# Hybrid decoder trunk on one core: a triangular solve's stores on ScalarE's queue, the bias table's columns from one wider load, x first in the first half

## The chip, the cores and the metric

The kernel runs on one core of a Trainium2 chip. The metric is the device time of one launch in microseconds (us), the median of several runs. A core has five engines that work side by side, each through its own list of instructions in order: TensorE (PE in the profile), VectorE (DVE), ScalarE (ACT), GpSimd (POOL) and SyncE (SP), which here does nothing but issue DMAs. An instruction whose input is not there holds up everything behind it on its engine, and that goes for a DMA issue too.

## The reference, cut to what matters

Two layers over 1024 tokens of width 1024. Each layer normalises x, projects it once, and splits the columns among four mixers; their outputs are gated, joined, projected, normalised and added to x.

```python
for i in range(DEPTH):
    h = rms_norm(x, g_pre[i])
    proj = h @ w_in[i]
    ...
    kc = nsa_compress(k_cmp, ...); vc = nsa_compress(v_cmp, ...)   # silu(flat @ w1) @ w2
    y_a = nsa_attention(q, kc, vc, ..., rel_bias)
    y_b = spatial_gating(u, v, ...)
    y_c = conv_module(glu_a, glu_b, ...)
    y_d = rwkv7_time_mix(token_shift(rw, mu), ...)      # a scan over tokens
    mix = concat([y_a * silu(z_a), y_b * silu(z_b), y_c * silu(z_c), y_d * silu(z_d)])
    x = x + rms_norm(mix @ w_out[i], g_post[i])
    x = x + sigmoid(x @ ple_gate[i]) * (p[i] @ ple_proj[i])
```

The recurrence of `rwkv7_time_mix` is computed here in chunks of 64 tokens. Each chunk needs the inverse of a 64 by 64 triangular matrix per head; that inverse is the "solve" of this document.

## The kernel before

**Halves and steps.** Each layer is done in two halves of 512 tokens, so there are four passes, called A, B, C and D here (layer 0 first and second half, layer 1 first and second half). `run` walks through a string of letters for each pass (`ORDER`, L32): X loads x, i and e do the embedding (`embed_in`, `embed_out`), H the norm, B `setup_late`, F and R the recurrence's front and its solve, N the front of the attention with the compression (`nsa_front`), r the recurrent steps, G, T and C the convolution, a, b, c, d the gates, s the spatial gating, A a tile of attention. The letters give the order in which the code is written; a tile scheduler then fixes the order of every engine's list, by priority and by its own idea of times.

**Weights.** Nearly all of TensorE's work is `mm3` (L169): three products of 128x512 for every 128x128 block of weights, with the high and low parts of both factors. Four blocks make a granule (12 products). `split_w` (L150) brings a granule: SP loads it to `ws` (L155), ScalarE rounds it to `wh` (L161), GpSimd subtracts for `wl` (L163), and where `keep` is set SP stores `wl` to memory (L166), so that the second half of the same layer loads it (L160) rather than have GpSimd do it again. All of this has three buffers, so SP can be about three granules ahead of TensorE.

**The solve** (`rwkv_solve`, L453). The triangular blocks go to a scratch tensor `Nd` and come back in another layout (L474, L479). VectorE then inverts 16x16 blocks by 15 pairs of small instructions (L487, L489), and the blocks below them by 16 more pairs (L509, L511). After the first group ScalarE copies a transposed `XT` (L495), and `put` (L497) stores 8 pieces in `Xd`; after the second it copies `WT` (L513), and `put` stores 8 more. All 16 stores are issued by SP (L499). `rwkv_tri` (L533) loads the finished chunks back (L539, SP) and begins with the products of L543.

**The compression** (`compress_out`, L866) is run beside the solve. Its products (L874) read eight tiles of `nsa_w1`, which SP loads to `ld` tiles (L834). There are five `ld` buffers, so five tiles come early and the last three can be loaded only when products have freed a buffer; the loads stand where the scheduler put them in SP's list.

**The bias table.** `setup_late` (L106) builds a table of biases by distance. It writes a scratch row, reads it back once as 128 overlapping rows of 256 (`hk`, L131), and reads every 16th element of it by four more DMAs (`hc`, L135), 128x17 single elements of 4 bytes each.

Of the kernel before, what the change touches and what calls it, by code (L numbers as in the profile page):

```python
# [16 lines left out]
TH = 512  # L17
NT = 4
KT = 8
# [9 lines left out]
C_ID, C_MA, C_ML, C_SUM, C_FAR, C_HB, C_FLAG, C_HS, C_N = 0, 128, 320, 384, 416, 544, 672, 673, 675  # L29
S_ANTI, S_OH, S_N = 0, 128, 256  # L30
RROW = 2128
ORDER = ("iXeHFBRNrGabscdnAAATCy",  # L32
         "HAFRNGrbsaAAAAdcniOexTgCy",
         "HFRNrGabscdniOxeAAgAATyC",
         "HFRNGraAbsAAnAcdOTxgCy")
# [6 lines left out]
class Trunk:  # L42
# [63 lines left out]
    def setup_late(self):  # L106
        nc, a = self.nc, self.a
        zz = self.t([128, 1024], "r4")
        nc.vector.memset(zz, 0.0)
        for i in range(2):  # L110
            for q in range(2):
                nc.sync.dma_start(self.Xd[i][:, q * 1024:q * 1024 + 1024], zz)

        rs = self.dram.tile([4, RROW], F32, name="rscratch")
        st = self.t([128, S_N], "r4")
        nc.sync.dma_start(st[:, :S_N], a["cst"][:, C_N:C_N + S_N])
        rb = self.const([32, 4], "rb")
        nc.sync.dma_start(rb, a["rel_bias"])
        row = self.t([128, 1024], "r4")
        row2 = self.t([128, 1024], "r4")  # L120
        nc.vector.memset(row[:4, :977], 0.0)
        nc.vector.memset(row2[:4, :1023], NEG)
        pr = self.ps("pt")
        nc.tensor.matmul(pr[:4, :128], rb, st[:32, S_OH:S_OH + 128], start=True, stop=True)
        mid = self.t([128, TH], "ld")[:4, :128]
        nc.vector.tensor_copy(mid, pr[:4, :128])
        nc.sync.dma_start(rs[:, :977], row[:4, :977])
        nc.sync.dma_start(rs[:, 977:1105], mid)
        nc.sync.dma_start(rs[:, 1105:2128], row2[:4, :1023])
        hk = self.t([128, 4, 256], "r4")  # L130
        nc.sync.dma_start(hk, bass.AP(tensor=rs.tensor, offset=rs.offset + 849,  # L131
                                      ap=[[1, 128], [RROW, 4], [1, 256]]))
        hc = self.t([128, TH], "ld")[:, :68].rearrange("p (a b) -> p a b", a=4)
        for h in range(4):
            nc.sync.dma_start(hc[:, h], bass.AP(tensor=rs.tensor, offset=rs.offset + 848 + h * RROW,  # L135
                                                ap=[[1, 128], [16, 17]]))
        for p in range(2):
            pj = self.ps("pt")
            nc.tensor.matmul(pj, st[:, S_ANTI:S_ANTI + 128],
                             hk[:, 2 * p:2 * p + 2, :].rearrange("p a b -> p (a b)"), start=True, stop=True)  # L140
            nc.scalar.copy(self.T[:, 2 * p:2 * p + 2, :].rearrange("p a b -> p (a b)"), pj)
        nc.vector.memset(self.TC[:, :, :53], 0.0)
        nc.vector.memset(self.TC[:, :, 70:], NEG)
        pj = self.ps("pt")
        nc.tensor.matmul(pj[:, :68], st[:, S_ANTI:S_ANTI + 128], hc.rearrange("p a b -> p (a b)"),
                         start=True, stop=True)
        nc.vector.tensor_copy(self.TC[:, :, 53:70], pj[:, :68].rearrange("p (a b) -> p a b", a=4))


# [303 lines left out]
    def rwkv_solve(self):  # L453
        nc = self.nc
        Nd, Xd = self.Nd[self.nq % 2], self.Xd[self.nq % 2]
        self.Xcur = Xd
        self.nq += 1
        self.AT, self.BKt, self.XF = {}, {}, {}
        for c in range(4):
            self.rwkv_ab(c)  # L460
            for j in range(2):
                nc.sync.dma_start(Nd[:, c * 256 + j * 128:c * 256 + j * 128 + 128].rearrange("p (h t) -> p h t", h=2),
                                  self.AT[c][0:64, j, :, 64 * j:64 * j + 64])
        ma = self.c[0:64, C_MA:C_MA + 64].unsqueeze(1).to_broadcast([64, 2, 64])
        for c in range(4, 8):
            Nc = self.t([128, 256], "q3", bufs=1)[:64].rearrange("p (a b c) -> p a b c", a=2, b=2)
            for e, pA in enumerate(self.a_blocks(1, c - 4, False)):
                nc.vector.tensor_mul(Nc[:, :, e], pA[0:64, :128].rearrange("p (h c) -> p h c", h=2), ma)
            nc.sync.dma_start(Nd[:, c * 256:c * 256 + 256].rearrange("p (h t) -> p h t", h=4),
                              Nc.rearrange("p a b c -> p (a b) c"))  # L470
        LB = self.t([128, 256], "q1", bufs=1).rearrange("p (a b) -> p a b", a=16)
        XB = self.t([128, 256], "q2", bufs=1).rearrange("p (a b) -> p a b", a=16)
        for b in range(4):
            nc.sync.dma_start(LB[b * 32:b * 32 + 32], bass.AP(tensor=Nd.tensor, offset=Nd.offset + b * 16 * 2048 + b * 16,  # L474
                                                              ap=[[64, 32], [2048, 16], [1, 16]]))
        L2 = self.t([128, 512], "l2", bufs=1).rearrange("p (a b) -> p a b", a=32)
        for b in range(4):
            p = b // 2
            nc.sync.dma_start(L2[b * 32:b * 32 + 32], bass.AP(  # L479
                tensor=Nd.tensor, offset=Nd.offset + p * 32 * 2048 + p * 32 + 16, ap=[[64, 32], [2048, 32], [1, 16]]))  # L480
        nc.gpsimd.memset(XB, 0.0)
        nc.gpsimd.affine_select(out=XB, in_=XB, compare_op=OP.not_equal, fill=1.0, base=0,
                                pattern=[[1, 16], [-1, 16]], channel_multiplier=0)
        tmp = self.t([128, 256], "q3", bufs=1)
        for t in range(1, 16):
            tv = tmp[:, :t * t].rearrange("p (a b) -> p a b", a=t)
            nc.vector.tensor_mul(tv, LB[:, 0:t, t].unsqueeze(1).to_broadcast([128, t, t]),  # L487
                                 XB[:, 0:t, 0:t].rearrange("p j a -> p a j"))
            nc.vector.tensor_reduce(XB[:, t, 0:t], tv, axis=AX.X, op=OP.add)  # L489
        XW = self.t([128, 32, 8], "q4", bufs=1)  # L490
        for b in range(4):
            p, g = divmod(b, 2)
            nc.vector.tensor_copy(XW[b * 32:b * 32 + 32, 0:16], XB[p * 64:p * 64 + 32, :, g * 8:g * 8 + 8])
        XT = self.t([128, 256], "q1", bufs=1).rearrange("p (a b) -> p a b", a=16)
        nc.scalar.copy(XT, XB.rearrange("p t j -> p j t"))  # L495

        def put(b, q, r0, c0, src, rows, cols):  # L497
            o = Xd.offset + (q * 64 + b // 2 * 32 + r0) * 2048 + b // 2 * 32 + c0
            nc.sync.dma_start(bass.AP(tensor=Xd.tensor, offset=o, ap=[[64, 32], [2048, rows], [1, cols]]),  # L499
                              src[b * 32:b * 32 + 32])  # L500

        for b in range(4):
            d = b % 2 * 16
            put(b, 0, d, d, XB, 16, 16)
            put(b, 1, d, d, XT, 16, 16)
        for t in range(16):
            n = 16 + t
            tv = tmp[:, :8 * n].rearrange("p (j a) -> p j a", j=8)
            nc.vector.tensor_mul(tv, L2[:, 0:n, t].unsqueeze(1).to_broadcast([128, 8, n]),  # L509
                                 XW[:, 0:n].rearrange("p a j -> p j a"))  # L510
            nc.vector.tensor_reduce(XW[:, n], tv, axis=AX.X, op=OP.add)  # L511
        WT = self.t([128, 128], "q5", bufs=1).rearrange("p (a b) -> p a b", a=8)
        nc.scalar.copy(WT, XW[:, 16:32].rearrange("p t j -> p j t"))  # L513
        for b in range(4):
            put(b, 0, 16, b % 2 * 8, XW[:, 16:32], 16, 8)
            put(b, 1, b % 2 * 8, 16, WT, 8, 16)
# [671 lines left out]
    def run(self):  # L1188
        prev = conv = att = None
        for l in range(2):  # L1190
            self.layer_setup(l)
            for h in range(2):
                self.h = h
                self.keep = h == 0
                mixd = self.mixd = self.mix_dram[h]
                for step in ORDER[2 * l + h]:
                    if step == "A":
# [13 lines left out]
                    elif step == "i":  # L1211
                        pT = self.embed_in()
                    elif step == "e":
                        self.embed_out(pT)
                    elif step == "X":
                        self.xs = [self.load_x(k) for k in range(KT)]
                    elif step == "n":
                        self.rwkv_norm()
                    elif step == "N":
# [106 lines left out]
```

## Time and profile before

| | |
|---|---|
| three runs | 1885.58, 1890.34, 1898.15 us; median 1890.34 |
| profiled execution, its own time | 1888.04 us |
| its span, first to last instruction | 1886.3 us |
| TensorE busy | 1700.9 us, 90% |
| VectorE, ScalarE, GpSimd busy | 1204.5, 798.0, 383.6 us |
| TensorE's mean granted clock | 0.934 of full speed |

The profile is one execution. In a timeline each row has its start, its duration, the engine, the line of the kernel, the operation, what it writes and reads, how many were merged, and in brackets how long the engine stood idle before it and what it waited for. PE is TensorE; SPq and ACTq are DMA issues of SyncE and ScalarE. The granted clock has two levels, 1.2 GHz (0.5 in the rows) and 2.4 GHz (1.00); a mean in between is a stretch with both.

### The profile page before, as it was taken

The page shows a single profiled execution, that of the slowest core. Times are in us where ns is not written, and L with a number is a line of the kernel's source. Part 1 is how long each engine was busy: PE and PEld are TensorE (multiplying, and loading weights), DVE is VectorE, ACT ScalarE, POOL GpSimd, SP SyncE. Part 2 cuts the span into 40 slices and gives each one's busy share as a digit, 9 for nine tenths or more (in the row PEclk, how much of TensorE's full clock was granted, in tenths as well). Part 3 has the DMA queues.
Part 4 walks back from the last instruction along what each step waited for, and adds up shares of the span by engine and source line. Part 5 has one row for each costly group of instructions (what it writes and reads, how often), then busy time and mean ns, then how long its engine had stood idle before and what let it go on. Part 6 is the DMA issues. An engine that isn't in the chain of part 4 may idle for free. (4 is left out here: it accounts for less than half of the span.)

```text
span 1886.3 us, 29258 instructions
## 1 busy us (share of the span) xinstructions
PE 1700.9 (90%) x10068; PEld 1252.8 (66%) x10068; DVE 1204.5 (64%) x3217; ACT 798.0 (42%) x1801; POOL 383.6 (20%) x319
## 2 busy tenths in 40 slices
PE   5795998999699999998877989999988999998998
PEld 4563676677576777775654768776766767675777
DVE  3456788765688764656566982557558877546353
ACT  4331233554223466544321334556432446554453
POOL 2222234000001023132331341200000011232333
PEclk8897798899899999998997989999998999989999
DMA  7645354324753443574464448672475424114554
GB/s 246 144 132 138 109 178 128 104 78 112 175 150 110 123 146 101 162 217 127 124 158 111 137 133 256 227 222 82 115 169 152 140 74 130 50 40 129 179 181 137
DMA packets 372492, 265.42 MB, mean 141 GB/s; under 512 B 93676, under 2 KB 305648, under 8 KB 372344
## 3 DMA queue, kind: packets, MB, share of 16 engines
q1 hardware_dynamic: 359288, 250.98, 46.7%
q10 hardware_dynamic: 13056, 12.59, 2.0%
q8 instruction: 79, 1.29, 0.3%
q14 instruction: 69, 0.57, 0.1%
HBM read 193.63 MB, written 69.86 MB: 140 GB/s over the span
## 5 line engine op out<-in xcount | busy, mean ns | idle before, releaser
L171 PE MATMUL mm<-aT,wh 128*128 128x512 f32 (+1 forms) x1304 | 540.2, 416 | 9.6 <-ACT aT L260 5.3
L172 PE MATMUL mm<-aT,wh 128*128 128x512 f32 (+1 forms) x1304 | 537.0, 412 | 3.8 <-DVE aT L261 3.2
L173 PE MATMUL mm<-aT,wl 128*128 128x512 f32 (+1 forms) x1304 | 535.4, 411 | 0.0
L161 ACT CAST wh<-ws 128x512 fp32r<-128x512 f32 (+2 forms) x388 | 236.7, 611 | 494.1 <-PE mm L172 313.3
L163 POOL TENSOR_TENSOR wl<-ws,wh 128x512 fp32r<-128x512 f32 (+1 forms) x220 | 292.0, 1329 | 702.1 <-ACT wh L161 647.1
L171 PEld LDWEIGHTS mm<-aT,wh 128*128 128x128 f32 (+1 forms) x1304 | 251.5, 193 | 70.8 <-ACT aT L260 7.8
L172 PEld LDWEIGHTS mm<-aT,wh 128*128 128x128 f32 (+1 forms) x1304 | 251.8, 193 | 62.7 <-DVE aT L261 11.0
L173 PEld LDWEIGHTS mm<-aT,wl 128*128 128x128 f32 (+1 forms) x1304 | 251.6, 193 | 51.1 <-issue 1.7
L697 DVE SCALAR_TENSOR_TENSOR cv<-cv,cw,cv 128x512 f32<-128x512 f32 x240 | 191.8, 808 | 4.0
L1035 ACT ACTIVATE r<-s,sma 128x512 f32<-128x512 f32 (+3 forms) x192 | 105.7, 554 | 52.7 <-DVE sma L1033 51.8
L976 ACT COPY pt<-pt 128x512 f32<-128x512 f32 (+1 forms) x152 | 80.4, 529 | 106.6 <-PE pt L973 106.2
L611 POOL TENSOR_TENSOR q<-SB,gc 128x256 f32<-128x256 f32 x28 | 22.9, 816 | 475.1 <-DVE SB L624 174.1
L973 PE MATMUL pt<-cst,r 128*128 128x128 f32 x528 | 102.9, 293 | 3.2 <-DVE r L1040 2.8
L981 PE MATMUL pv<-pt,vs 128*64 128x128 f32 x1056 | 93.4, 291 | 3.7 <-ACT pt L976 3.5
L981 PEld LDWEIGHTS pv<-pt,vs 128*64 128x64 f32 x1056 | 55.8, 138 | 57.3 <-ACT pt L976 47.5
L973 PEld LDWEIGHTS pt<-cst,r 128*128 128x128 f32 x528 | 61.2, 143 | 38.4 <-issue 23.9
L1025 DVE CUSTOM_DVE_ANT_0 s<-s,T 128x256 f32<-128x256 f32 (+1 forms) x144 | 54.2, 377 | 46.4 <-PE s L1006 45.8
L1005 PE MATMUL s<-kv,qs 128*128 128x512 f32 (+2 forms) x192 | 74.6, 390 | 3.0 <-ACT r L1035 2.9
L874 PE MATMUL pt<-ld,t 128*32 128x128 f32 x256 | 13.0, 330 | 67.0 <-DMA ld<-in_nsa_w_dram 67.0
L1040 DVE TENSOR_SCALAR r<-r,sma 128x640 f32<-128x640 f32 (+7 forms) x128 | 68.3, 533 | 0.7
L1006 PE MATMUL s<-kv,qs 128*128 128x512 f32 (+2 forms) x192 | 65.7, 347 | 0.0
L1037 DVE TENSOR_TENSOR sma<-sma 128x1 f32<-128x1 f32 x64 | 13.7, 214 | 70.1 <-ACT r L1035 69.9
(328 smaller groups left out, 2687.2 us busy)
## 6 DMA issues: line engine op xcount, KB each, us to landing
ws<-in_w_in_dram SPq DMA_DIRECT2D x232, 256.0 KB, 3.2
wl<-low SPq DMA_DIRECT2D x164, 256.0 KB, 2.7
low<-wl SPq DMA_DIRECT2D x148, 256.0 KB, 2.1
ws<-in_ple_gate_dram SPq DMA_DIRECT2D x64, 256.0 KB, 3.0
ws<-in_w_out_dram SPq DMA_DIRECT2D x60, 256.0 KB, 2.9
ped<-ot ACTq DMA_DIRECT2D x32, 256.0 KB, 4.2
ld<-in_nsa_w_dram SPq DMA_DIRECT2D x32, 256.0 KB, 3.1
ld<-ped SPq DMA_DIRECT2D x32, 256.0 KB, 3.8
```

Source lines behind the costliest of these rows:

```text
L161: nc.scalar.copy(hi[:, :cols], st[:, :cols])
L163: nc.gpsimd.tensor_sub(lo[:, :cols], st[:, :cols], hi[:, :cols].bitcast(F32))
L171: nc.tensor.matmul(out, lh, rh, start=first, stop=False, skip_group_check=shared)
L172: nc.tensor.matmul(out, lh, rl, start=False, stop=False, skip_group_check=shared)
L173: nc.tensor.matmul(out, ll, rh, start=False, stop=last, skip_group_check=shared)
L697: nc.vector.scalar_tensor_tensor(ac, xg[j][:, k:k + TH], cw[:, j * 31 + k:j * 31 + k + 1], ac, op0=OP.mult, op1=OP.add)
L973: nc.tensor.transpose(pt[:, o:o + 128], P[e][:, (b + x - b0) * 128:(b + x - b0) * 128 + 128], self.ident)
L976: nc.scalar.copy(PT[:, :n], pt[:, :n])
L981: nc.tensor.matmul(acc[e], w.VS[hh][:, tt, br], PT[:, o:o + 128], start=False, stop=br == 1 and b + x == i, skip_group_check=True)
L1005: nc.tensor.matmul(p[:, :n], w.QS[hd][:, qs], w.KH[br, hh][:, c0 * 128:c1 * 128], start=True, stop=False)
L1035: nc.scalar.activation(P[:, o:o + wd], p[:, c:c + wd], AF.Exp, bias=ng[:, 0:1], accum_out=den[:, x:x + 1])
L1040: nc.vector.tensor_scalar(P[:, :n], P[:, :n], r, None, op0=OP.mult)
```

## The change

The 64 stores of the four solves are issued by ScalarE. `hk` is loaded one element wider, both tables are read from it, and the four loads of single elements are gone. In pass A the step X stands before i, its loads are given high priority, and `embed_out` runs with `keep` off, so that the low parts of `ple_proj` are not stored, and are computed by GpSimd each time.

```diff
-ORDER = ("iXeHFBRNrGabscdnAAATCy",
+ORDER = ("XieHFBRNrGabscdnAAATCy",
...
-        hk = self.t([128, 4, 256], "r4")
-        nc.sync.dma_start(hk, bass.AP(tensor=rs.tensor, offset=rs.offset + 849,
-                                      ap=[[1, 128], [RROW, 4], [1, 256]]))
-        hc = self.t([128, TH], "ld")[:, :68].rearrange("p (a b) -> p a b", a=4)
-        for h in range(4):
-            nc.sync.dma_start(hc[:, h], bass.AP(tensor=rs.tensor, offset=rs.offset + 848 + h * RROW,
-                                                ap=[[1, 128], [16, 17]]))
+        hk = self.t([128, 4, 257], "r4")
+        nc.sync.dma_start(hk, bass.AP(tensor=rs.tensor, offset=rs.offset + 848,
+                                      ap=[[1, 128], [RROW, 4], [1, 257]]))
...
-                             hk[:, 2 * p:2 * p + 2, :].rearrange("p a b -> p (a b)"), start=True, stop=True)
+                             hk[:, 2 * p:2 * p + 2, 1:257], start=True, stop=True)
...
-        nc.tensor.matmul(pj[:, :68], st[:, S_ANTI:S_ANTI + 128], hc.rearrange("p a b -> p (a b)"),
-                         start=True, stop=True)
+        nc.tensor.matmul(pj[:, :68], st[:, S_ANTI:S_ANTI + 128], hk[:, :, 0:257:16], start=True, stop=True)
...
-            nc.sync.dma_start(bass.AP(tensor=Xd.tensor, offset=o, ap=[[64, 32], [2048, rows], [1, cols]]),
-                              src[b * 32:b * 32 + 32])
+            nc.scalar.dma_start(bass.AP(tensor=Xd.tensor, offset=o, ap=[[64, 32], [2048, rows], [1, cols]]),
+                                src[b * 32:b * 32 + 32])
...
                     elif step == "e":
+                        self.keep = False
                         self.embed_out(pT)
+                        self.keep = h == 0
                     elif step == "X":
-                        self.xs = [self.load_x(k) for k in range(KT)]
+                        with self.tc.high_priority():
+                            self.xs = [self.load_x(k) for k in range(KT)]
```

The scheduler orders the whole program anew, so the lists differ in many places. Three of them follow, all in pass A's solve; passes B, C and D look alike. In the changed kernel's rows the line numbers are 5 lower.

SP's list in the kernel before: the second eight of the solve's stores (`Xd<-q`, L499; the first eight stand just above) and the last three loads of the compression's weights (`ld<-in_nsa_w_dram`, L834):

```order
L834 DMA ld_1309<-in_nsa_w_dram 128x4x128
L499 DMA Xd_85<-q_217_966 32x16x8
L499 DMA Xd_85<-q_219_1013 32x8x16
L499 DMA Xd_85<-q_217_966 32x16x8
L499 DMA Xd_85<-q_219_1013 32x8x16
L499 DMA Xd_85<-q_217_966 32x16x8
L499 DMA Xd_85<-q_219_1013 32x8x16
L499 DMA Xd_85<-q_217_966 32x16x8
L499 DMA Xd_85<-q_219_1013 32x8x16
L834 DMA ld_1315<-in_nsa_w_dram 128x4x128
L834 DMA ld_1321<-in_nsa_w_dram 128x4x128
```

SP's list in the changed kernel, from the last loads of the solve's input (`l<-Nd`, now L474) on:

```order
L474 DMA l_214_913<-Nd_83 32x32x16 x2
L829 DMA ld_1296<-in_nsa_w_dram 128x4x128
L161 DMA low_1894<-wl_1891 128x512
L150 DMA ws_1954<-in_w_in_dram 128x4x128
L829 DMA ld_1302<-in_nsa_w_dram 128x4x128
L161 DMA low_1918<-wl_1915 128x512
L150 DMA ws_1974<-in_w_in_dram 128x4x128
L829 DMA ld_1308<-in_nsa_w_dram 128x4x128
L747 DMA ld_2174<-in_sgu_wT_dram 128x4x128
```

The three loads have moved ahead of everything that waits for the solve; nine granules' loads (`ws`), two of them in these rows, stand between the solve's input and the first `x<-Xd` (L534).

ScalarE's list before, from `XT`'s copy to `WT`'s:

```order
L495 COPY q_218_971<-q_214_921 128x256
L161 CAST wh_1927<-ws_1925 128x512
L161 CAST wh_1947<-ws_1945 128x512
L161 CAST wh_1969<-ws_1967 128x512
L513 COPY q_219_1013<-q_217_966 128x128
```

ScalarE's list in the changed kernel around `WT`'s copy (L508) and the second group of stores (L494); the first group stands further up between three casts of granules:

```order
L156 CAST wh_2021<-ws_2019 128x512
L508 COPY q_218_1000<-q_216_953 128x128
L494 DMA Xd_85<-q_216_953 32x16x8
L494 DMA Xd_85<-q_218_1000 32x8x16
L494 DMA Xd_85<-q_216_953 32x16x8
L494 DMA Xd_85<-q_218_1000 32x8x16
L156 CAST wh_2045<-ws_2043 128x512
L494 DMA Xd_85<-q_216_953 32x16x8
L494 DMA Xd_85<-q_218_1000 32x8x16
L494 DMA Xd_85<-q_216_953 32x16x8
L494 DMA Xd_85<-q_218_1000 32x8x16
L156 CAST wh_2065<-ws_2063 128x512
```

The copy now stands three casts of granules later in the list than before, and the casts of the next two granules stand behind it and the stores.

VectorE's list before, at the end of the solve:

```order
L509 TENSOR_TENSOR q_216_935<-l_215_926,q_217_966 128x240
L511 TENSOR_REDUCE q_217_966<-q_216_935 128x8
L509 TENSOR_TENSOR q_216_935<-l_215_926,q_217_966 128x248
L511 TENSOR_REDUCE q_217_966<-q_216_935 128x8
L682 SCALAR_TENSOR_TENSOR cv_1834<-t_382_1837,mm_1880 128x512
```

VectorE's list in the changed kernel at the same place (L692 is a tap of the convolution, L697 before; L504 and L506 are L509 and L511):

```order
L692 SCALAR_TENSOR_TENSOR cv_3357<-cv_1821,cw_99,cv_3357 128x512
L504 TENSOR_TENSOR q_215_922<-l_214_913,q_216_953 128x240
L692 SCALAR_TENSOR_TENSOR cv_3357<-cv_1821,cw_99,cv_3357 128x512
L506 TENSOR_REDUCE q_216_953<-q_215_922 128x8
L692 SCALAR_TENSOR_TENSOR cv_3357<-cv_1821,cw_99,cv_3357 128x512
L504 TENSOR_TENSOR q_215_922<-l_214_913,q_216_953 128x248
L692 SCALAR_TENSOR_TENSOR cv_3357<-cv_1821,cw_99,cv_3357 128x512
L506 TENSOR_REDUCE q_216_953<-q_215_922 128x8
```

Taps and other work of the convolution and the compression have come between the last pairs of the solve.

On TensorE the number of weight products (L171 to L173) between the place at which pass A's compression waits and the first product on the solve's result (L543) is 0 before and 82 now; in B it is 0 and 78, in C 0 and 82, in D 48 and 90. In B only the first two of L543's products stand at that place.

## Rows read from the trace of the kernel before

**Rows 1.** The page: busy us, share, instructions; GB/s in 40 slices.

```profile
PE 1700.9 (90%) x10068; PEld 1252.8 (66%) x10068; DVE 1204.5 (64%) x3217; ACT 798.0 (42%) x1801; POOL 383.6 (20%) x319
...
GB/s 246 144 132 138 109 178 128 104 78 112 175 150 110 123 146 101 162 217 127 124 158 111 137 133 256 227 222 82 115 169 152 140 74 130 50 40 129 179 181 137
```

**Rows 2.** Who waited for whom: us in total, times, longest.

```profile
ACT q L513 <- DVE q L511: 45.1, 4, 12.8
...
PE pt L874 <- DMA ld<-in_nsa_w_dram: 67.0, 12, 12.2
```

**Rows 3.** Timeline of TensorE in pass A: start us, us, what.

```profile
161.25 0.39 PE L173 MATMUL mm<-aT,wl 128*128 128x512 f32 x1
...
163.97 0.39 PE L173 MATMUL mm<-aT,wl 128*128 128x512 f32 x1
174.85 0.66 PE L874 MATMUL pt<-ld,t 128*32 128x128 f32 x8 [10.49 <-DMA ld<-in_nsa_w_dram]
187.69 0.66 PE L874 MATMUL pt<-ld,t 128*32 128x128 f32 x8 [12.19 <-DMA ld<-in_nsa_w_dram]
...
190.69 0.69 PE L543 MATMUL rp<-x,at 64*64 64x64 f32 x8
```

**Rows 4.** Timeline of SP's DMA issues over the same stretch.

```profile
153.58 1.16 SPq L479 DMA_DIRECT2D l<-Nd  x2
...
171.97 0.43 SPq L834 DMA_DIRECT2D ld<-in_nsa_w_dram  x1
180.61 3.92 SPq L499 DMA_DIRECT2D Xd<-q  x8
184.63 0.95 SPq L834 DMA_DIRECT2D ld<-in_nsa_w_dram  x2
...
186.30 0.84 SPq L539 DMA_DIRECT2D x<-Xd  x2
```

**Rows 5.** Timeline of VectorE: the solve's last instruction in passes A to D.

```profile
180.17 0.41 DVE L511 TENSOR_REDUCE q<-q 128x8 f32<-128x248 f32 x1
...
505.38 0.41 DVE L511 TENSOR_REDUCE q<-q 128x8 f32<-128x248 f32 x1
...
994.10 0.41 DVE L511 TENSOR_REDUCE q<-q 128x8 f32<-128x248 f32 x1
...
1421.59 0.41 DVE L511 TENSOR_REDUCE q<-q 128x8 f32<-128x248 f32 x1
```

**Rows 6.** Windows: length, each engine's busy us (instructions), clock, DMA share, GB/s.

```profile
164.40:209.80 45.40, 22.07 (x111) 13.72 (x111) 25.93 (x55) 4.64 (x12) 7.01 (x6) 0.55 0.48 120
498.30:523.90 25.60, 10.94 (x51) 6.91 (x51) 12.89 (x27) 2.91 (x9) 1.54 (x2) 0.53 0.48 120
978.80:1015.40 36.60, 13.99 (x80) 8.39 (x81) 21.01 (x47) 3.52 (x10) 5.38 (x5) 0.53 0.53 128
1410.40:1428.40 18.00, 7.46 (x42) 4.73 (x42) 14.18 (x32) 2.09 (x7) 0.61 (x1) 0.62 0.57 118
83.00:100.60 17.60, 7.78 (x31) 5.11 (x31) 4.77 (x12) 5.37 (x9) 4.16 (x3) 0.61 0.80 238
```

**Rows 7.** Timeline of SP, then of TensorE, at the bias table.

```profile
65.10 12.47 SPq L135 DMA_DIRECT2D ld<-rscratch  x4
...
92.86 1.86 PE L386 MATMUL rp<-cst,t 128*128 128x2 f32 x8 [9.82 <-ACT t L383]
```

**Rows 8.** Timeline of TensorE at the start: the first norm.

```profile
31.92 1.86 PE L268 MATMUL mm<-onec,qa 128*128 128x1 f32 x8 [8.28 <-DVE qa L301]
```

**Rows 9.** Groups on the page: line, engine, operation, count, busy us, mean ns, idle before.

```profile
L161 ACT CAST wh<-ws 128x512 fp32r<-128x512 f32 (+2 forms) x388 | 236.7, 611 | 494.1 <-PE mm L172 313.3
L163 POOL TENSOR_TENSOR wl<-ws,wh 128x512 fp32r<-128x512 f32 (+1 forms) x220 | 292.0, 1329 | 702.1 <-ACT wh L161 647.1
...
L697 DVE SCALAR_TENSOR_TENSOR cv<-cv,cw,cv 128x512 f32<-128x512 f32 x240 | 191.8, 808 | 4.0
```

**Rows 10.** Timeline of TensorE: a link of the recurrent steps.

```profile
281.19 0.46 PE L602 MATMUL c<-q,xf 64*64 64x64 f32 x8 [2.01 <-DVE q L599]
```

## The prediction

> **What bounds the kernel now.** I read the page first, then the list of waits, then timelines of single stretches. TensorE is busy 90% of the span [rows 1], so what can be won is its idle time, some 185 us, and the time it works at the lower clock. The list of waits names one cause that stands out: TensorE waited 67.0 us, 12 times, for tiles of `nsa_w1` [rows 2].
>
> The timelines of pass A tell why. TensorE works without a break to 164.4, then waits 10.49 and 12.19 us for two tiles that L874 multiplies [rows 3]. SP had issued the solve's input at 153.6 and the first of the three late tiles only at 172.0, the other two at 184.6 [rows 4]. What stands between in its list are the stores of the solve. The second eight are issued at 180.61, right behind VectorE's last instruction of the solve (180.17 + 0.41) [rows 4, 5]. So the loads waited for VectorE, with which they have nothing to do, because SP issues in order. TensorE waits in its turn and drops to the lower clock.
>
> Windows from the stall's start to the clock's return, for A to D, give the size [rows 6]. Length less PE busy is 45.4 - 22.1 = 23.3, 25.6 - 10.9 = 14.7, 36.6 - 14.0 = 22.6 and 18.0 - 7.5 = 10.5 us, 71.1 us idle in all. The busy parts, 22.1, 10.9, 14.0 and 7.5 us, lie nearly all behind the stall, where the granted clock was 0.50; at full clock half of that time would do, so the clock costs up to 27.2 us more.
>
> A smaller place lies in the front. The four loads of single elements hold SP for 12.47 us from 65.1; the weights behind them come late and TensorE waits 9.82 us at 83 [rows 7]. That window has 9.8 us idle and 7.8 us busy, mostly at 0.50: 9.8 + 3.9 = 13.7 us [rows 6].
>
> **The stores on ScalarE: what goes.** SP's list in the changed kernel has the three tiles behind the solve's input and ahead of what waits for the solve, so they need only a free buffer, which TensorE's first products on the tiles give. I count the waits for `nsa_w1` as gone.
>
> What is late next is the solve itself. In pass A the first product on its result (L543) starts at 190.69 [rows 3], 10.1 us behind VectorE's end at 180.58: copy, eight stores (3.92 us of issue), their landing, and the load of `x` [rows 4, 5]. On ScalarE the same eight stores stand behind `WT`'s copy with one cast of weights among them (0.61 us [rows 9]). ScalarE's price of issuing such a store isn't in the trace. The nearest row is SP's, 3.92 / 8 = 0.49 us; from nothing to double that is 0 to 8 us per solve, and I take 0.49. So 10.7 us from VectorE's end to L543.
>
> VectorE's end moves too. In its new list the last pairs of A are mixed with six taps of the convolution and six smaller instructions: 6 x 0.81 [rows 9] = 4.9, and some 2 us for the others (an estimate from L511's 0.41 us [rows 5], since they are as small), 6.8 us; in B and D seven taps, 7.6 us. If all of it fell into gaps of the pairs it would be 0, if each waited for its input more; I take the full sum. L543 can then start at 180.6 + 6.8 + 10.7 = 198.1 in A; with the ends of the other passes [rows 5], 505.8 + 7.6 + 10.7 = 524.1 in B, 994.5 + 6.8 + 10.7 = 1012.0 in C, and 1422.0 + 7.6 + 10.7 = 1440.3 in D.
>
> Against this stands the work that TensorE now has before L543. From the old stall on these are 82, 78, 82 and 90 weight products. Twelve of them take 163.97 - 161.25 = 2.72 us [rows 3], 0.227 each, so 18.6, 17.7, 18.6 and 20.4 us. The compression's own small products add an estimated 3.8 us (three groups of 0.66 [rows 3], and as much again), and 1.2 us in B for a group of the solve's. TensorE is ready at 164.4 + 18.6 + 3.8 = 186.8 in A, 498.3 + 17.7 + 5.0 = 521.0 in B, 978.8 + 18.6 + 3.8 = 1001.2 in C and 1410.4 + 20.4 + 3.8 = 1434.6 in D. It waits 11.3, 3.1, 10.8 and 5.7 us, 30.9 us in all. In A and C part of that comes a little sooner, because the casts of the last granule before L543 stand behind `WT`'s copy; that splits the wait and does not add to it.
>
> Idle time saved: 71.1 - 30.9 = 40.2 us. The work pulled forward is paid for by leaving less work for later; nothing is done twice.
>
> Clock: three waits over 5 us stay. The one wait of this size in the front cost 3.9 us of clock, so I leave 3 x 3.9 = 11.7 of the 27.2 us and save 15.5. The bounds are 0, if the clock falls for as long as now, and 27.2, if it doesn't fall.
>
> What is queued behind the new waits: on ScalarE the casts of the following granules. ScalarE already waits 45.1 us in its four copies L513 [rows 2]; that copy now stands three granules later, about when VectorE ends. The stores themselves add no wait, as each stands behind a copy that waited for the same tile.
>
> A rule of the Trainium skill speaks against this part: "DMA: Bandwidth & Descriptors", section "Issuing engines are not separate DMA queues", says that DMAs from any engine end on the same 16 DMA engines, and that spreading them saves only the issuing sequencer's time. By it alone 64 x 0.49 = 31 us of SP's time is saved, none of it on TensorE's path, and the stores are worth nothing. The trace agrees that issue time is small but shows that here SP's list is held by waits, which the rule leaves out [rows 4].
>
> **The bias table.** The four loads go, and with them the 12.47 us of SP. The wide load is one element wider per row; I cost it at nothing. The new slice of `hk` feeds one product of 68 columns. Saved 13.7 us; at least 9.8 if the clock falls for another reason. What comes next there is TensorE's own chain through ScalarE and VectorE.
>
> **x first.** The eight loads of x (2 MB) now stand ahead of those of p, which feed TensorE's first products. At the 246 GB/s of the first slice [rows 1] that is 8 us of later start. The cover is the 8.28 us for which TensorE waits in front of the first norm, because x is late [rows 8]: the norm's products stand behind the embedding in TensorE's list, so they start as early as before, at about 32 us, and the wait moves to the front. I take 0, with bounds of 8 us lost and 8 us gained. With `keep` off GpSimd subtracts for 8 more granules, 8 x 1.33 = 10.6 us [rows 9], and 16 DMAs of 256 KB go. GpSimd is busy 20% of the span [rows 1], one subtraction takes half of a granule's 2.72 us of products, and the loads run three granules ahead: 0, at worst 10.6.
>
> **Sum.** 40.2 + 15.5 + 13.7 = 69.4 us. The profiled execution took 1888.0 us, 2.3 under the median of 1890.3, so 1888.0 - 69.4 = 1818.6, and I say 1819.
>
> **Rivals.**
> 1. The waits move to ScalarE. If VectorE ends its mixed chain later than I think, ScalarE stands in L513 as it does now, 11.3 us on average, the casts behind it starve TensorE, and each pass wins nothing. For it: TensorE has only three granules of weights ahead. Against it: 82 products take twice that wait. Only the front's gain is left: 1888.0 - 13.7 = 1874. 0.05. The same 1874 follows if the loads were late for another reason than SP's list, full DMA engines for one, so that the stores save issue time alone; the engines' share of busy time is about half in these windows [rows 6], so 0.02. This second case is the one that the rule of the Trainium skill quoted above would lead to.
> 2. Slower: the recurrent steps run dry. The 82 products and more that now come before the steps no longer fill them. Each step has three links from TensorE over a copy and back; where few products stand between, the link costs 2.01 us [rows 10]. With 32 steps there are 96 links. It decides against the change from 70 / 96 = 0.73 us more per link; at 2 us in half of them it is 96 us, 1819 + 96 = 1915. For it: a scheduler's times were wrong about the solve. Against it: the new list pulls other work (spatial gating, the first attention tile) between the links. 0.04.
> 3. No wait is left at the solves and the clock holds: 71.1 + 27.2 + 13.7 = 112, 1776. For it: B is nearly there. Against it: VectorE's end is fixed by 31 pairs that nothing shortens. 0.12.
>
> **How the numbers follow.** My forecast has 0.77. Its range follows from its unknowns: the clock 15 down and 12 up, ScalarE's issue 8 in three passes, x first and the subtractions some 8 each, hardly all one way: 1786 to 1852. It leaves out most of rivals 1 to 3. About 1%, 19 us, is what a measurement of this kernel can tell from no change. Rival 1 with its 0.07 is 0.7% under before, so it counts as no change; rival 2 is slower; the rest is faster: 0.89, 0.07, 0.04.
>
> **What would show it.** Right: no wait of L874 for `nsa_w1`; a wait of 3 to 11 us at the first product on the solve's result in each pass; taps of the convolution inside the solve on VectorE; the 9.82 us at 83 gone; the first norm near 32 us. Wrong: ScalarE waiting over 10 us in L513's copy with TensorE idle behind its casts; idle time spread over the links of the steps; the first norm at 40 us.

## The result and the profile after

The changed kernel takes 1814.57 us (median of 4 runs, 1811.26 to 1819.83) against 1888.39 us (4 runs). The ratio is 0.9603, 95% interval 0.956 to 0.9645: 75 us faster. 1819 was predicted, with 1786 to 1852 as the range. The profiled execution is the slowest of the four: 1819.83 us, span 1818.1 us, 68.2 us shorter than before.

The head of the page of the changed kernel answers to [rows 1]:

```profile
span 1818.1 us, 29200 instructions
PE 1687.8 (93%) x10068; PEld 1242.4 (68%) x10068; DVE 1208.3 (66%) x3217; ACT 797.0 (44%) x1801; POOL 402.8 (22%) x327
```

TensorE's work is the same 10068 instructions. Span less busy was 1886.3 - 1700.9 = 185.4 us and is 130.3 now: 55.1 us less idle. Its busy time fell by 13.1 us with the same work: that is the clock, whose mean rose from 0.934 to 0.961.

The list of waits of the changed kernel (who waited for what: us in all, times, longest), against [rows 2]:

```profile
PE mm L166 <- ACT t L1060: 18.9, 1, 18.9
...
PE pt L869 <- DMA ld<-in_nsa_w_dram: 15.9, 9, 4.3
ACT wh L156 <- DMA Xd<-q: 15.6, 8, 3.0
...
PE rp L538 <- DMA x<-Xd: 9.6, 4, 4.7
...
ACT q L508 <- DVE q L506: 7.2, 3, 3.3
...
PE pt L135 <- DMA r<-rscratch: 6.2, 1, 6.2
```

Four readings (the first row, 18.9 us, is the start, which stands later because x is loaded first; it was 9.5 before). TensorE's waits for `nsa_w1` (L874, now L869) fell from 67.0 to 15.9 us. Its wait for the solve's result (L538) has appeared, 9.6 us. ScalarE's wait in `WT`'s copy (45.1 us before) has not grown but shrunk to 7.2, as the copy stands later in its list. Its casts wait 15.6 us behind the stores that it issues now.

Windows over the four solves, from the first wait to the clock's return, as [rows 6] has them of before, and under them the stretches at the lower clock that lie in them (length, PE busy, PEld, DVE, ACT, POOL, granted clock, DMA share, GB/s):

```profile
150.40:192.00 41.60, 30.80 (x142) 22.89 (x142) 40.46 (x71) 10.04 (x21) 16.05 (x11) 0.84 0.67 171
466.90:496.00 29.10, 26.63 (x140) 20.30 (x140) 27.81 (x57) 8.27 (x18) 1.26 (x2) 1.00 0.89 239
924.50:973.70 49.20, 39.75 (x179) 28.36 (x178) 44.10 (x79) 11.25 (x23) 16.95 (x12) 0.79 0.62 162
1348.90:1362.70 13.80, 10.50 (x53) 6.72 (x53) 11.62 (x29) 2.49 (x8) 1.49 (x2) 0.63 0.83 233
157.90:164.70 6.80, 5.10 (x23) 3.35 (x23) 6.46 (x15) 1.10 (x3) 2.16 (x2) 0.50 0.83 237
185.20:192.00 6.80, 4.55 (x23) 3.28 (x24) 6.68 (x12) 0.62 (x1) 1.27 (x1) 0.50 0.53 147
929.30:932.70 3.40, 2.81 (x7) 1.65 (x5) 3.19 (x7) 0.50 (x1) 1.37 (x1) 0.50 0.97 235
936.10:939.50 3.40, 3.40 (x12) 2.25 (x11) 3.33 (x10) 0.38 (x2) 1.58 (x1) 0.50 0.49 133
960.00:973.70 13.70, 12.71 (x60) 8.44 (x60) 9.61 (x19) 1.83 (x3) 3.24 (x2) 0.50 0.35 108
1352.50:1362.70 10.20, 9.30 (x43) 6.14 (x43) 8.30 (x21) 1.87 (x7) 1.49 (x2) 0.50 0.71 210
```

Length less PE busy is 10.8, 2.5, 9.5 and 3.3 us in A to D, 26.0 in all, where it was 71.1. At the lower clock TensorE worked 37.9 us (the six lower rows), which costs half of it, 19 us, where it was 27.2. So the solves give 45.1 us of idle time and 8.2 of clock. Up to the solve of pass A, `XT`'s copy there stands at 150.7 instead of 162.6, which is 11.9 us for the front. 45.1 + 8.2 + 11.9 = 65.2 of the 68.2 us; the last 3 are scattered.

### The profile page after: what moved, and what is told of

Its sections match the earlier page's. It is cut to its first block, busy times and chain, and to the rows that moved or that the text cites. A ratio compares the mean times of both kernels' runs of the same rounds, so it can differ in the third digit from the quotient of the medians.

```text
span 1818.1 us, 29200 instructions
## 1 busy us (share of the span) xinstructions
PE 1687.8 (93%) x10068; PEld 1242.4 (68%) x10068; DVE 1208.3 (66%) x3217; ACT 797.0 (44%) x1801; POOL 402.8 (22%) x327
## 5 line engine op out<-in xcount | busy, mean ns | idle before, releaser
L158 POOL TENSOR_TENSOR wl<-ws,wh 128x512 fp32r<-128x512 f32 (+1 forms) x228 | 308.8, 1356 | 704.3 <-ACT wh L156 596.5
L692 DVE SCALAR_TENSOR_TENSOR cv<-cv,cw,cv 128x512 f32<-128x512 f32 x240 | 200.3, 850 | 2.3
L1110 DVE SCALAR_TENSOR_TENSOR ot<-ot,ld 128x512 f32<-128x512 f32 x24 | 25.1, 1048 | 50.3 <-ACT ot L1109 45.3
```

The lines of the kernel that those rows point to most:

```text
L158: nc.gpsimd.tensor_sub(lo[:, :cols], st[:, :cols], hi[:, :cols].bitcast(F32))
L692: nc.vector.scalar_tensor_tensor(ac, xg[j][:, k:k + TH], cw[:, j * 31 + k:j * 31 + k + 1], ac, op0=OP.mult, op1=OP.add)
```

## The experiments

**Theory 1.** The loads of `nsa_w1` were late because they stood in SP's list behind stores that waited for VectorE. **Rival.** They were late for issue time or full DMA engines, or what SP holds up above all is the granules. Two later theories stand with their runs.

All edits are against the kernel named; "idle" is span less PE busy of the profiled execution. The kernel before was timed again beside each group of runs; its four medians are the range in the first row, and each ratio is to the one taken beside the run.

| run | time, us | ratio to before, 95% | idle, us | mean clock | PE waits for `nsa_w1` |
|---|---|---|---|---|---|
| before | 1886.99 to 1890.9 | | 185.4 | 0.934 | 67.0 |
| changed kernel | 1814.57 | 0.9603 (0.956 to 0.9645) | 130.3 | 0.961 | 15.9 |
| stores_only | 1826.27 | 0.9667 (0.9642 to 0.9693) | 139.0 | 0.959 | 16.8 |
| table_only | 1879.61 | 0.9938 (0.9912 to 0.9964) | 177.2 | 0.934 | 67.8 |
| x_first | 1889.02 | 1.0003 (0.9979 to 1.0027) | 189.6 | 0.935 | 66.9 |
| loads_on_act | 1852.07 | 0.9803 (0.9775 to 0.983) | 145.1 | 0.947 | 10.6 |
| own_buffers | 1843.76 | 0.9759 (0.9732 to 0.9785) | 147.8 | 0.948 | 0 |
| third_part_undone | 1810.69 | 0.9595 (0.9569 to 0.9621) | 128.8 | 0.962 | 18.0 |
| after_own_buffers | 1815.27 | 0.9597 (0.957 to 0.9625) | 138.0 | 0.967 | 0 |
| after_loads_on_act | 1826.24 | 0.9683 (0.9645 to 0.9721) | 143.2 | 0.962 | 11.7 |
| low_on_pool | 1846.38 | 0.9788 (0.9764 to 0.9812) | 146.8 | 0.955 | 12.0 |
| stores_on_pool | 1872.94 | 0.9925 (0.9896 to 0.9953) | 175.5 | 0.949 | 23.3 |

**stores_only: the first part alone**, in the kernel before.

```diff
-            nc.sync.dma_start(bass.AP(tensor=Xd.tensor, ...
+            nc.scalar.dma_start(bass.AP(tensor=Xd.tensor, ...
```

> The kernel before with one part of the change alone: the 64 stores of the solves issued by ScalarE. Theory 1 (SP's list was held by stores that waited for VectorE, and the compression's loads stood behind them): the waits for nsa_w1 fall from 67 us to under 20, idle 40 us and clock 15 us less, so about 1833 us, 55 under the kernel before; the 9.82 us at 83 and the 8.28 us before the first norm stay. Rival (only the issue time of the stores is saved, the loads are late for another reason): 1888 us with waits for nsa_w1 of 60 us or more. Rival (the waits move to ScalarE): 1888 us, with the idle time in front of weight products and ScalarE over 40 us in its copies of WT.

0.9667 of 1890.9 us: 63 us, between 58 and 68. Waits for `nsa_w1` 16.8 us; the 10.1 us at 83 and the 8.1 us before the first norm are still there. The first product on the solve's result in A starts at 198.4; 198.1 was worked out. That this is within 0.3 us is in part luck: `XT`'s copy stands 1.7 us later than before, and the pairs took 23.5 us from there instead of the 24.8 worked out. Theory 1 holds; the rival that the waits move to ScalarE falls.

**table_only: the second part alone**, the diff's lines in `setup_late`.

> The kernel before with the bias table's part alone: one wider load, four loads of single elements gone. As predicted: the 9.82 us at 83 and its clock go, 13.7 us, about 1875 us. Rival, from the changed kernel's trace, where the product behind the wide load waits 6.25 us at 36: the wait for the scratch row comes back at another place, and 9.82 - 6.25 = 3.6 us are left, with some clock 1880 to 1885 us.

11.7 us (7 to 17). The wait at 83 is gone and no wait for the scratch row has come in its place; `XT`'s copy in pass A stands at 149.9 instead of 162.6, 12.7 us sooner. The prediction's price of 13.7 us lies within what the runs leave open. Over the whole span the profile shows less, 8.4 us: idle time fell by 8.2 and TensorE's busy time only from 1700.9 to 1700.7, so the 3.9 us of clock are not seen there. The 6.2 us that the changed kernel's L135 waits for the row come with the third part: x_first waits 6.9 us at the same product.

**x_first: the third part alone**, the diff's lines in `ORDER` and `run`.

> The kernel before with the third part alone: x loaded first with high priority, and the embedding's low parts not kept. As predicted: nothing, 1888 us, the first product at about 19 us instead of 9.5 and the 8.28 us before the first norm gone. Rival: the later start isn't given back, 8 to 10 us slower, 1897 us. Rival: TensorE, which starts late but then works without a break, loses no clock there (the half-clock stretch of 13.7 us from 28.9 goes), up to 7 us faster, 1881 us.

Nothing: 1.0003. TensorE starts at 18.9 us, no longer waits before the norm, and the norm stands at 32.6 (31.9 before). But behind it a wait of 6.9 us for the bias table's scratch row comes, and 5.2 of the old 9.82 us are left.

**loads_on_act: the loads moved and not the stores.** If Theory 1 is right, it doesn't matter which of the two leaves SP's list.

```diff
-        self.nc.sync.dma_start(w.rearrange("p (l m) -> p l m", l=4), self.a["nsa_w1"]...
+        self.nc.scalar.dma_start(w.rearrange("p (l m) -> p l m", l=4), self.a["nsa_w1"]...
```

> The kernel before with its stores left on SP; only the issues of the compression's weight loads (nsa_w1) are moved, to ScalarE, where pass A's last three stand ahead of the copy of XT. Theory 1 (SP's list held by waits makes the loads late): the waits for nsa_w1 fall under 20 us although no store has moved, and 20 to 55 us are won (1833 to 1868); what is left of the idle time is then behind granules, whose loads still stand behind the stores in SP's list. Rival (the issue time or full DMA engines made the loads late, so that the stores had to leave SP): waits for nsa_w1 stay at 60 us, 1888 us.

37 us won (32 to 43) with all 64 stores where they were, and waits for `nsa_w1` of 10.6 us. The loads still fall beside the solve, which speaks against full DMA engines.

**own_buffers: neither moved to another engine.** The last three tiles are loaded early, so that nothing has to be issued during the solve.

```diff
-        self.w1 = [self.load_w1(x) for x in range(5)]
+        self.w1 = [self.load_w1(x) for x in range(8)]
...
-        w = self.t([128, TH], "ld")
+        w = self.t([128, TH], "ld") if x < 5 else self.ot()
```

> The kernel before with its stores left on SP; the last three tiles of nsa_w1 get buffers of their own (the three ot buffers, which no other tile needs at that time) and are loaded with the first five, long before the solve. Theory 1 (the loads were late because they stood in SP's list behind stores that waited for VectorE): the waits for nsa_w1 go, from 67 us to under 5, with every store where it was, and the time comes near to that of the stores on ScalarE alone (1826): 1825 to 1855, since granules still stand behind the stores in SP's list. Rival (what SP's stores hold up above all is the granules, and the loads were only the first to show it): TensorE then waits as long for weight products, 1880 us or more.

The longest waits of TensorE's list in this kernel (same view as above):

```profile
PE pt L973 <- DVE r L1040: 12.4, 14, 2.4
PE pt L880 <- ACT t L877: 10.9, 4, 4.1
PE mm L171 <- ACT t L1065: 10.0, 1, 10.0
PE rp L386 <- ACT t L383: 9.8, 1, 9.8
PE mm L268 <- DVE qa L301: 8.4, 1, 8.4
PE mm L171 <- DVE cv L682: 7.7, 3, 4.3
```

No row for `nsa_w1` is left, and 45.6 us are won, with every store and every issue still SP's. So it was not SP's issue time either, but the place in the list: Theory 1 is shown twice over. Each edit has the scheduler order every list anew (in loads_on_act the pairs of A end 31.5 us behind `XT`'s copy instead of 18.0), so the waits show the cause, while the time won also holds what each new order brought or cost. What this kernel lacks of stores_only is 17 us, 20.9 by the profiled spans. Idle time is 8.8 us of those; the other 12.1 are busy time and go with the clock, whose mean is 0.948 against 0.959. Its lower stretches lie in many places with little idle time in them, and why they fell so I can't say.

**stores_on_pool: a third engine for the stores**, in the changed kernel.

```diff
-            nc.scalar.dma_start(bass.AP(tensor=Xd.tensor, ...
+            nc.gpsimd.dma_start(bass.AP(tensor=Xd.tensor, ...
```

> The changed kernel, with the solves' stores issued by GpSimd instead of ScalarE. Theory 1 (any list will do that doesn't hold up loads or weights for longer than three granules, 8.2 us): ScalarE's casts are no longer held behind stores, but GpSimd's subtractions in passes A and C are, while in B and D the low parts come from memory; 1810 to 1830 us, waits for nsa_w1 under 20 us. Rival: stores from GpSimd take much longer to issue or to land, so the first product on the solve's result comes later, by 8 us or more in each pass: 1850 us. Rival (ScalarE's queue is what matters): 1888 us.

Missed: 1873 us, 58 slower than on ScalarE by the medians. The timeline of GpSimd in pass A's solve (start, us, engine, line, operation):

```profile
149.40 0.87 POOL L494 DMA_DIRECT2D Xd<-q  x1 [3.72 <-DVE q L484]
152.04 0.67 POOL L494 DMA_DIRECT2D Xd<-q  x1 [1.77 <-issue]
154.46 0.65 POOL L494 DMA_DIRECT2D Xd<-q  x1 [1.76 <-issue]
155.13 1.28 POOL L158 TENSOR_TENSOR wl<-ws,wh 128x512 fp32r<-128x512 f32 x1
156.88 0.67 POOL L494 DMA_DIRECT2D Xd<-q  x1 [0.48 <-issue]
```

The stores follow each other at best every 2.42 us (154.46 - 152.04, 156.88 - 154.46), though each counts only 0.65 and a subtraction fits in between. SP needs 0.49 for one [rows 4]. The first product on the solve's result then starts 18.1 to 20.9 us behind VectorE's end instead of 10.3 to 13.1, and TensorE waits 33.4 us there. The rival that only ScalarE's queue would do is not borne out: the price is GpSimd's own, and it was the rival with the longer issue that came true, with more than its 1850.

**third_part_undone: the changed kernel with x and `keep` as before.**

> The changed kernel without its third part (x first, embedding's low parts not kept), that is, the kernel before with the stores on ScalarE and the wider load. Theory 1 with parts that add up: 1890.9 less the 63 and 11.7 us that the two parts brought alone, 1816 us, the same as the changed kernel within 1%. Rival: x first is worth something only in company, for its price is hidden by a wait that the others remove; then this kernel is 8 us or more faster (1807) or slower (1823) than the changed one.

0.9595 beside 0.9603: no worth of the third part can be told in company either, though the two intervals leave some 9 us open either way. The two other parts add up, 63 + 11.7 = 75.

**Theory 2**, on the 15.9 us of waits for `nsa_w1` that are left. In pass A of the changed kernel, timelines of ScalarE, SP and TensorE:

```profile
150.68 0.62 ACT L490 COPY q<-q 128x256 f32<-128x256 f32 x1 [4.80 <-DVE q L484]
...
151.74 0.62 ACT L156 CAST wh<-ws 128x512 fp32r<-128x512 f32 x1 [0.44 <-ACT q L490]
...
148.19 0.51 SPq L829 DMA_DIRECT2D ld<-in_nsa_w_dram  x1
154.00 0.34 SPq L161 DMA_DIRECT2D low<-wl  x1
154.45 0.37 SPq L150 DMA_DIRECT2D ws<-in_w_in_dram  x1
154.94 0.49 SPq L829 DMA_DIRECT2D ld<-in_nsa_w_dram  x1
...
159.19 0.65 PE L869 MATMUL pt<-ld,t 128*32 128x128 f32 x8 [4.35 <-DMA ld<-in_nsa_w_dram]
```

ScalarE stands 4.80 us for VectorE in `XT`'s copy, as it did in the kernel before (4.83). What is new is that a load hangs on it: the cast behind the copy is late, so is GpSimd's subtraction, and the store of that low part holds SP until 154.00, with the load of `nsa_w1` behind it. Three kernels tried to break this chain.

**low_on_pool**, the stores of the low parts issued by GpSimd:

```diff
-                nc.sync.dma_start(kept, lo[:, :cols].bitcast(F32))
+                nc.gpsimd.dma_start(kept, lo[:, :cols].bitcast(F32))
```

> The changed kernel, with the stores of the low parts (140 of 256 KB) issued by GpSimd, each right behind the subtraction that makes it, and no longer by SP. Theory 2, on what is left: ScalarE stands 4.8 us in XT's copy for VectorE, its next cast is late, GpSimd's subtraction too, the store of that low part heads SP's list, and the load of nsa_w1 stands behind it; 15.9 us of waits for nsa_w1 are left. If so, they fall under 6 us here, and 10 us of idle time and some clock go: 1800 us. Rival: these loads are late because their buffers are; then the waits stay at 16 us and the time at 1815. Rival: issuing on GpSimd costs its subtractions so much that they fall behind TensorE's granules (1.36 of 2.72 us are taken now); then TensorE waits for wl, 1830 us or more.

Missed, and 32 us slower than the changed kernel by the medians. The waits fell only to 12.0: in A the 4.35 us became 1.19, but an earlier one is 2.40. That load was issued at 139.56, behind the load of a granule at 139.07, which started when GpSimd's subtraction had ended (139.04); the last product on its buffer's old tile had ended at about 138.2. So SP's list still hangs on GpSimd, now by the granules' buffers. The price on GpSimd:

```profile
L161 POOL DMA_DIRECT2D low<-wl x144 | 82.3, 572 | 56.2 <-POOL wl L158 55.8
```

0.57 us of issue and 0.39 us before it, 144 times. What turned this into 32 us isn't settled: the idle time is 16.5 us more and lies in small waits for VectorE and ScalarE in many places, where the scheduler's order is another too.

**after_loads_on_act**, the edit of loads_on_act in the changed kernel:

> The changed kernel, with the loads of nsa_w1 issued by ScalarE too, in pass A ahead of XT's copy. Theory 2 gives waits for nsa_w1 under 8 us and 8 us of idle time less, 1806 us. Rival: what these waits no longer hold back comes later, at the first product on the solve's result, whose time VectorE sets: 1815 us with 8 us more idle time there.

Missed: the waits fell to 11.7 us, not under 8, and the kernel is slower than the changed one, 0.9683 beside 0.9603. TensorE waits instead behind ScalarE and VectorE in the compression (3.0 and 3.8 us at L883 in A and C) and once for a scaled q (3.1 us).

**after_own_buffers**, the edit of own_buffers in the changed kernel, which puts **Theory 3** to the test: VectorE sets the solve's end, so that what TensorE no longer waits for `nsa_w1` it waits for later.

> The changed kernel with the same own buffers for the last three tiles of nsa_w1. Theory 3 (VectorE's end sets the first product on the solve's result): the 15.9 us of waits for nsa_w1 that are left go to 0, but in passes A and C they come back at that product (4.7 and 3.75 us there now, then 8 to 10); only B's and D's 3.6 us and some clock are won, 1806 to 1814 us. Rival (TensorE's own work sets it): all 15.9 us and some 5 us of clock are won, 1794 us.

The waits for `nsa_w1` are gone and the time is the same, 1815.27, 1 us above the range of Theory 3; its rival with 1794 falls. But Theory 3's mechanism is not borne out. The waits at L538 in A and C did not grow to 8 to 10 us; they are 2.5 and 2.3, and 8.0 in all (9.6 before). Instead 12.0 us came at L875, in the compression, 4.09 of them in A. In the timelines of VectorE, ScalarE and TensorE:

```profile
143.17 0.69 DVE L822 SCALAR_TENSOR_TENSOR qs<-mm,qs 64x512 fp32r<-64x512 f32 x1
...
143.89 0.59 ACT L821 ACTIVATE qs<-mm 64x512 fp32r<-64x512 f32 x1 [4.70 <-DVE qs L822]
144.51 0.37 ACT L872 COPY t<-pt 128x256 f32<-128x256 f32 x1
...
144.93 0.63 PE L875 MATMUL pt<-cst,t 128*128 128x32 f32 x4 [4.09 <-ACT t L872]
```

This wait lies 30 us ahead of VectorE's end (174.9): the early tiles have moved the compression ahead of the solve's second group, the copy that TensorE needs stands in ScalarE's list behind the scaling of a q, and that waits for VectorE's part of the scaling (L822), which stands among the pairs of the solve. It is the same cause once more, on other lists. Idle time rose to 138.0, and the clock, at 0.967, made up for it.

**two_taps**, in the changed kernel:

```diff
-            for k in range(1, 31):
+            for k in range(1, 2):
```

> The changed kernel with 2 of the convolution's 31 taps, so 232 of 240 instructions of VectorE (0.85 us each) are left out; its time is no measure of the change. Step 1 of the prediction, taps mixed into the solve's last pairs delay VectorE's end by 4.9 us of 6.8: from XT's copy to the end of the pairs VectorE took 25.6, 22.1, 25.1 and 23.4 us in passes A to D (18.0, 16.5, 17.5 and 17.0 before the change); without taps it is about 20 in each, and the waits at the first product on the solve's result (4.7 and 3.75 us in A and C) fall to 0 to 1 us. Rival (the pairs are slower for another reason, GpSimd's subtractions beside them): still 24 us and more in A and C, and the waits stay.

From `XT`'s copy to VectorE's end it took 21.8, 19.6, 21.9 and 20.2 us: 2.5 to 3.8 us less than with taps, about half of what the change had added. About 20 us was expected, and B and D show it; A and C don't. There five subtractions lie in the stretch, and the 16 products take 12.3 and 12.5 us instead of 10.4 and 9.9 before: GpSimd is worth some 2 to 2.6 us there (last section), so the rival was right in part. In B and D no subtraction lies in it; what is left above the kernel before, 3.1 and 3.2 us, is the one tap that is kept, small instructions of other steps, and gaps. The waits at L538 did not go (3.2, 1.9, 3.0, 2.0 us): fewer products stand before it in this kernel's list, so that TensorE is ready sooner as well.

## Why the prediction was right, step by step

| step | predicted, us | measured, us | by |
|---|---|---|---|
| idle at the solves, what remains | 11.3, 3.1, 10.8, 5.7 | 10.8, 2.5, 9.5, 3.3 | windows |
| idle saved at the solves | 40.2 | 45.1 | windows |
| clock saved there | 15.5 | 8.2 | windows |
| stores, both together | 55.7 | 53.3; alone 63 (58 to 68) | windows; stores_only |
| bias table | 13.7 | 11.7 (7 to 17) | table_only |
| x first, `keep` off | 0 | -0.6 (-5 to 4) | x_first |
| sum | 69.4 | 68.2 of span; 75 by runs | |

The mechanism was right. That the sums agree to 1.2 us of span is luck: idle time at the solves came out 4.9 us better, the clock there 7.3 us worse and the front 1.8 us worse (11.9 for 13.7), and some 3 us are scattered.

**The stores.** The step that carried the forecast, that SP's list was held by waits and not by work, is shown by own_buffers and loads_on_act. The Trainium skill's rule that spreading DMAs over issuing engines saves issue time alone ("DMA: Bandwidth & Descriptors", section "Issuing engines are not separate DMA queues") would have left stores_only and loads_on_act at 1888. The runs differ from it, at 1826 and 1852 us, and the measurement decides. own_buffers, which moves no issue to another engine, won as well (1844).

**VectorE's end and L543.** From `XT`'s copy to VectorE's end the pairs took 18.0, 16.5, 17.5 and 17.0 us; now 25.6, 22.1, 25.2 and 23.3. That is 7.6, 5.6, 7.7 and 6.3 more, predicted 6.8 and 7.6 in turn. In A and C the 16 products were 2.1 and 1.0 us longer than before, beside six of GpSimd's subtractions instead of three, which the sum had left out. From there to the first product it took 11.1, 10.3, 10.7 and 13.1 us, predicted 10.7 (in D TensorE itself was not ready sooner). ScalarE's issue of a store, which no row showed, has a median of 0.45 us; 0.49 was taken.

**Where it failed.** "I count the waits for `nsa_w1` as gone": 15.9 us are left, by Theory 2's chain and the five buffers. With them TensorE comes later to the solve's result, and waits there only 4.7, 0.8, 3.8 and 0.4 us instead of 11.3, 3.1, 10.8 and 5.7; so two of the signs, no such wait and 3 to 11 us at L543 in each pass, failed. The two errors cancel: 26.0 us idle against 30.9. In A and C, where the product starts 11.1 and 10.7 us behind VectorE's end, an earlier TensorE would have waited longer at L543, so VectorE's end seems to fix the sum; that is read from this trace alone, and after_own_buffers did not bear it out.

**The clock** was the mis-sized term. I left it 3.9 us per wait over 5 us. The waits are shorter and more (each under 5 us), yet it fell behind nearly all of them: in A after 1.35 + 4.35 us from 150.6 on and after 4.7 at 182.8, in C after 3.2 and 2.2 at 925 and 932 and after 3.75 at 957, in D even after the 2.4 us at 1349. In B, whose waits were 1.18 and 0.79 us, it held. So it cost 19 us at the solves, not 11.7. In all TensorE's busy time fell by 13.1 us, where the sum had 15.5 + 3.9 = 19.4; 5.6 of the 13.1 lie ahead of pass A's `XT` copy (busy 126.0 before, 120.4 now).

**The rivals.** Waits that move to ScalarE: 7.2 us in `WT`'s copy, not 45, and 13.0 in `XT`'s copy, which waited 13.1 before. Steps that run dry: TensorE's idle time at the lines of the recurrent steps, L538's wait left out, was 8.9 us and is 7.7. No waits and a clock that holds: only B did that. The first norm stands at 33.4 us (near 32 was foretold, 40 would have been wrong).

## What to carry to other kernels

When an engine waits for a load, look at what stands ahead of that load's issue in its queue's list: one store whose data is late holds all that follows, and three cures (move the store, move the load, load it earlier into an idle buffer) each won 37 to 63 us here. Then look for the next late thing before removing what is left: taking away the last 15.9 us won nothing (after_own_buffers), as 12.0 us of waits came up behind ScalarE's list instead, and in A that stood behind VectorE's.

## What the runs showed of the hardware

GpSimd spaces the first eight of a solve's stores, 512 pieces of 64 bytes each, at best 2.42 us apart (stores_on_pool), while a store of 128 rows of 2 KB costs it 0.57 us (low_on_pool). ScalarE's median over all 64 of the solves' stores is 0.45 us.

VectorE's products of the solve stand still while GpSimd subtracts. In pass A of the changed kernel, the timelines of GpSimd and VectorE:

```profile
167.01 1.34 POOL L158 TENSOR_TENSOR wl<-ws,wh 128x512 fp32r<-128x512 f32 x1 [4.66 <-ACT wh L156]
...
167.11 1.72 DVE L504 TENSOR_TENSOR q<-l,q 128x232 f32<-128x232 f32 x1
...
169.41 0.39 DVE L506 TENSOR_REDUCE q<-q 128x8 f32<-128x232 f32 x1
```

The product began 0.10 us behind the subtraction, which ended at 168.35, and ended 0.48 us after that; in the kernel before the same product, with no subtraction beside it, took 0.58. Of the 64 products of L504, the 16 that overlap a subtraction took 0.97 us on average and the 48 others 0.51; the reductions behind them (L506), with one input, took 0.32 (6 that overlap one) and 0.35. The Trainium skill says so ("SBUF — State Buffer", section "SBUF: two separate sides"): a GpSimd instruction that reads SBUF (the memory on the chip that holds these tiles) and a VectorE instruction with two inputs from it exclude each other for a whole instruction. The trace agrees. So a subtraction, which the prediction counted as free, can cost VectorE 1.1 us, and it counts where it falls beside the solve's pairs, as six do in A and in C (three before the change).
